# Four heads of a gated recurrence in step instead of two, in a two-layer hybrid decoder

## The chip, the core and the metric

The kernel runs on one core of one Trainium2 chip. The metric is the device time of one execution, in microseconds (us). The core has a matrix engine (TensorE, PE in the profile; its weight loads are listed as PEld), a vector engine (VectorE, DVE), a scalar engine (ScalarE, ACT), a general engine (GpSimd, POOL) and a queue that issues transfers (SyncE, SP). Each takes its own instructions in order, and they wait for one another through semaphores. SBUF is the memory that all of them read; PSUM is what TensorE writes, eight banks of 512 fp32 columns in 128 partitions.

## What is computed

Two layers over 512 tokens of width 1024. Each layer normalises its input, projects it to 6400 columns, runs two groups of heads side by side, gates both with SiLU, projects back and adds:

```python
h = rms_norm(x, g_pre)
q_h, f_h, i_h, z_h, q_a, k_a, v_a, z_a = jnp.split(h @ w_in, SPLIT_POINTS, axis=-1)
o_h = hgrn2(q_h, f_h, i_h, lb)                  # 8 heads, state 128 x 128
o_h = rms_norm(o_h, g_head) * jax.nn.silu(z_h)
o_a = sliding_window_attention(rotary(q_a), rotary(k_a), v_a, sinks) * jax.nn.silu(z_a)
x = x + rms_norm(jnp.concatenate([o_h, o_a]) @ w_out, g_post)
```

The recurrence of a head, which the change touches, is

```python
f = lb + (1 - lb) * sigmoid(f_logit);  k = 1 - f;  q = silu(q)
S_t = diag(f_t) S_{t-1} + k_t i_t^T;   o_t = S_t^T q_t
```

Everything is fp32. The large matmuls split each operand into a high and a low part and add three products.

## The kernel before

**Projections.** The weight columns come in slabs of 512: QA (2 slabs, attention queries), IV (2, the recurrence's i), FQ (4; slab FQ+p holds f and q of heads 2p and 2p+1), ZA and ZH (2 each, the gates), and the output weights in four parts a0, a1, h0, h1. `ORDER` gives their order in a layer. Each slab is cut into units that accumulate in one PSUM bank each (`pj`, three banks). A unit of an input slab has 8 steps, one of an output slab 4; a step is three 128x512 matmuls at L282. Two units run at a time, step by step in turn; `begins` says when the next one may start. When a unit ends, its `evac` reads the bank: for FQ, sigmoid, its complement and two scalings per f head (L646 to L649) and a SiLU per q head (L655); for ZA, SiLU (L798), product with the attention output (L799), high part (L800), low part (L801).

**Weights.** Each piece of 128x512 is loaded through SP's queue (L156), its high part made by ScalarE (L176), its low part by VectorE (L177; a few by GpSimd). `plan_conversions` walks the units ahead of time and gives each piece the step at which it is due.

**The recurrence.** `hgrn(a)` does the pair of heads a and a+1. It first prepares both: reciprocals, products, copies (L671 to L681). Then come six levels, for blocks of hh = 2, 4, ..., 64 tokens. In a level TensorE multiplies q of the right half of each block with k of the left half, in small matmuls that write 32 or 64 partitions each (L703 for hh up to 16, L709 for 32, L714 for 64; each is two instructions in the profile, since fp32 takes two passes). Then VectorE scales q (L720), GpSimd scales k (L721), both by the running products `tots`, and the results are kept in the score tile A: masked copies on VectorE for hh up to 16 (L732), ScalarE copies above. The diagonal blocks of two tokens (L690, kept at L727) go in with the first level. After the levels k is transposed (L750), chunk states are summed (L760 to L764), and the outputs are made (L772, L775) and normalised (L778 to L782). `a_tiles`, two score tiles cleared once at the start, serve all pairs.

**Order.** `merge` interleaves the recurrence with projection steps in the program: a stream advances when it has done the smaller share of its total. The recurrence's generator yields weights, 28.5 in all per pair (`HG_N`): 3.5 per prepared head, 2.0 or 2.5 per level, 2.0 after the transposes, 1.5 per state, 2.0 per output. The four pairs are merged with the slabs up to FQ+1, FQ+2, a1 and h0. The compiler then orders each engine's instructions by readiness; small matmuls are pinned (`pin`) behind everything written before them on TensorE, large ones are not. `sc()` hands out three PSUM banks in turn for the recurrence's and attention's scores, `ac()` two more for states and outputs. SBUF tiles come from pools by tag: `fk` has 8 tiles for f and k, `q` 4 for pairs of q, `b` and `a` 2 of double width, `s` 3, `u` 1.

Of the kernel before, what the change touches and what calls it, by code (L numbers as in the profile page):

```python
# [17 lines left out]
D_MODEL = 1024  # L18
# [11 lines left out]
QA, IV, FQ, ZA, ZH = 0, 2, 4, 8, 10  # L30
FEATURE = (0, 1, 4, 5, 6, 7, 8, 9)
# [3 lines left out]
HG_N = 28.5  # L35
# [32 lines left out]
def hybrid_kernel(ctx: ExitStack, tc: tile.TileContext, x, wkv, win, wout, g_pre, g_post, lbp, ghead, sinks,  # L68
# [19 lines left out]
    sc_turn = [0]  # L88
# [5 lines left out]
    def ac():  # L94
        return ps.tile([P, 512], F32, tag="ac", name="ac", bufs=8 - PJ - SC)
# [28 lines left out]
    ORDER = ["kv", QA, QA + 1, IV, IV + 1, FQ, ZA, FQ + 1, "a0", FQ + 2, ZA + 1, FQ + 3, "a1", ZH, "h0", ZH + 1, "h1"]  # L124
# [301 lines left out]
    def layer(l, last):  # L426
# [213 lines left out]
        def fq_stream(p):  # L640
            def evac(m, o):
                h = 2 * p + m % 2
                if m < 2:
                    f = big.tile([P, 512], F32, tag="fk", name="f", bufs=FB)
                    k = big.tile([P, 512], F32, tag="fk", name="k", bufs=FB)
                    nc.scalar.activation(f, o, AF.Sigmoid)  # L646
                    nc.scalar.activation(k, o, AF.Sigmoid, scale=-1.0)
                    nc.scalar.activation(f, f, AF.Identity, scale=lb_a[:, l, h:h + 1], bias=lb_b[:, l, h:h + 1])
                    nc.scalar.activation(k, k, AF.Identity, scale=lb_a[:, l, h:h + 1], bias=lb_c[:, l, h:h + 1])  # L649
                    fT[h], kT[h] = f, k  # L650
                else:
                    if m == 2:
                        qT["t"] = big.tile([P, 2, 512], F32, tag="q", name="q", bufs=QB)
                    qT[h] = qT["t"][:, m - 2]
                    nc.scalar.activation(qT[h], o, AF.Silu)  # L655
# [6 lines left out]
        def hgrn(a):  # L662
            hs = [(j, fT.pop(a + j), kT.pop(a + j), qT.pop(a + j), a_tiles[j]) for j in range(2)]
            blocks = lambda t, w: t.rearrange("p (b j) -> p b j", j=w)
            qbs, kbs, tots = [], [], []
            for j, f, k, q, A in hs:
# [3 lines left out]
                re = halves("a")[0][:, 0:256]  # L670
                nc.vector.reciprocal(re, f2[:, :, 1])  # L671
# [3 lines left out]
                nc.vector.tensor_tensor(kb2[:, :, 1], k2[:, :, 1], re, op=ALU.mult)  # L675
                qbs.append(qb)
                kbs.append(kb)
# [4 lines left out]
                tots.append(f2[:, :, 0])  # L682
                yield 3.5
            LBs = []
            for j in range(2):
                LB = sc()
                for n in range(NT):
                    for b in range(4):
                        c = slice(n * P + 32 * b, n * P + 32 * b + 32)
                        pin(nc.tensor.matmul(LB[32 * b:32 * b + 32, c], lhsT=kbs[j][:, c], rhs=qbs[j][:, c], start=True, stop=True,  # L690
                                             tile_position=(0, 32 * b)))
                LBs.append(LB)
            for hh in (2, 4, 8, 16, 32, 64):
                nb = SEQ // (2 * hh)
                per, qu = nb // NT, nb // NT // 4
                L = sc()
                for j, f, k, q, A in hs:
                    qv = q.rearrange("p (b two j) -> p b two j", two=2, j=hh)
                    if hh <= 16:
                        for n in range(NT):  # L700
                            for b in range(4):
                                o_, blk, c = n * P + 32 * b, n * per + b * qu, 256 * j + n * 64 + 16 * b
                                pin(nc.tensor.matmul(L[32 * b:32 * b + 32, c:c + 16], lhsT=k[:, o_:o_ + 32],  # L703
                                                 rhs=qv[:, blk:blk + qu, 1, :], start=True, stop=True, tile_position=(0, 32 * b)))
                    elif hh == 32:
                        for n in range(NT):
                            for b in range(2):
                                o_, r_, c = n * P + 64 * b, 64 * b + 32 * (n % 2), 64 * j + n // 2 * 32
                                pin(nc.tensor.matmul(L[r_:r_ + 32, c:c + 32], lhsT=k[:, o_:o_ + 32],  # L709
                                                 rhs=q[:, o_ + 32:o_ + 64], start=True, stop=True, tile_position=(0, r_)))  # L710
                    else:
                        for n in range(NT):
                            o_, b, c = n * P, n % 2, 128 * j + n // 2 * 64
                            pin(nc.tensor.matmul(L[64 * b:64 * b + 64, c:c + 64], lhsT=k[:, o_:o_ + 64],  # L714
                                             rhs=q[:, o_ + 64:o_ + 128], start=True, stop=True))
                for j, f, k, q, A in hs:
                    qv = q.rearrange("p (b two j) -> p b two j", two=2, j=hh)
                    kv_ = k.rearrange("p (b two j) -> p b two j", two=2, j=hh)
                    tv = tots[j].rearrange("p (b two) -> p b two", two=2)
                    nc.vector.tensor_tensor(qv[:, :, 1, :], qv[:, :, 1, :], tv[:, :, 0].unsqueeze(2).broadcast_to([P, nb, hh]), op=ALU.mult)  # L720
                    nc.gpsimd.tensor_tensor(kv_[:, :, 0, :], kv_[:, :, 0, :], tv[:, :, 1].unsqueeze(2).broadcast_to([P, nb, hh]), op=ALU.mult)  # L721
                    t2 = sm.tile([P, nb], F32, tag=f"tot{hh}", name=f"tot{hh}", bufs=2)
                    nc.vector.tensor_tensor(t2, tv[:, :, 0], tv[:, :, 1], op=ALU.mult)
                    tots[j] = t2
                for j, f, k, q, A in hs:
                    if hh == 2:
                        nc.vector.copy_predicated(A.rearrange("p (n t) -> p n t", n=NT), bmask.unsqueeze(1).broadcast_to([P, NT, P]),  # L727
                                                  LBs[j].rearrange("p (n t) -> p n t", n=NT))
                    if hh <= 16:
                        Av = A.rearrange("p (n b two j) -> p n b two j", n=NT, two=2, j=hh)[:, :, :, 1, :]  # L730
                        mv = lmask[hh].rearrange("p (b j) -> p b j", j=hh).unsqueeze(1).broadcast_to([P, NT, per, hh])
                        nc.vector.copy_predicated(Av, mv, L[:, 256 * j:256 * j + 256].rearrange("p (n b j) -> p n b j", n=NT, j=hh))  # L732
                    elif hh == 32:
                        Av = A.rearrange("p (m two t) -> p m two t", m=NT // 2, two=2)
                        for b in range(2):
                            for i in range(2):
                                nc.scalar.copy(Av[64 * b:64 * b + 32, :, i, 64 * b + 32:64 * b + 64],
                                               L[64 * b + 32 * i:64 * b + 32 * i + 32, 64 * j:64 * j + 64].rearrange("p (m t) -> p m t", m=NT // 2))
                    else:
                        Av = A.rearrange("p (m b t) -> p m b t", m=NT // 2, b=2)  # L740
                        for b in range(2):
                            nc.scalar.copy(Av[0:64, :, b, 64:128],
                                           L[64 * b:64 * b + 64, 128 * j:128 * j + 128].rearrange("p (m t) -> p m t", m=NT // 2))
                yield 2.5 if hh == 2 else 2.0

            kps = []
            for j, f, k, q, A in hs:
# [6 lines left out]
            yield 2.0  # L754
            vs = lambda j, n: vt[a // 4, n][:, (a % 4 + j) * P:(a % 4 + j + 1) * P]
            sts = []
            for j, f, k, q, A in hs:
# [5 lines left out]
                for n in range(1, NT - 1):  # L763
                    nc.vector.scalar_tensor_tensor(st[:, n], st[:, n - 1], tots[j][:, n:n + 1], SU[:, n * P:(n + 1) * P],  # L764
                                                   op0=ALU.mult, op1=ALU.add)
                sts.append(st)
                yield 1.5
            for j, f, k, q, A in hs:
# [15 lines left out]
                yield 2.0  # L784
# [128 lines left out]
        def run():  # L913
            hg = lambda a: (hgrn(a), HG_N)
# [110 lines left out]
    a_tiles = [const.tile([P, 512], F32, name=f"a_st{i}") for i in range(2)]  # L1025
# [4 lines left out]
    def constants():  # L1030
# [10 lines left out]
        for t in a_tiles:  # L1041
            pin(nc.gpsimd.memset(t, 0.0))
# [41 lines left out]
def _layout(inp):  # L1084
# [6 lines left out]
    fq = np.stack([f_h.reshape(DEPTH, D_MODEL, 4, 256), q_h.reshape(DEPTH, D_MODEL, 4, 256)], axis=3).reshape(DEPTH, D_MODEL, 2048)  # L1091
# [28 lines left out]
```

## Time and profile before

| | |
|---|---|
| median of 3 runs | 934.13 us (933.86 to 934.25) |
| profiled execution | 933.88 us, its span 932.1 us |
| PE busy | 910.0 us, 98% |
| DVE, ACT, POOL busy | 72%, 50%, 29% |
| granted TensorE clock, mean | 0.994 |
| large matmuls (L282), share of the chain that ended last | 71% |

The span is the time from the first to the last instruction. A row of the timeline has the start, the time from the start to the last end of its merged instructions, engine, line, operation, tiles (out<-in), shape, and xcount. Matmuls are pipelined, so one starts before the last has ended, and the spacing of starts tells what each costs. A row of a group has the busy time, the mean of one in ns, and the idle time before, with what ended it.

### The profile page before, as it was taken

The page shows a single profiled execution, that of the slowest core. Times are in us where ns is not written, and L with a number is a line of the kernel's source. Part 1 is how long each engine was busy: PE and PEld are TensorE (multiplying, and loading weights), DVE is VectorE, ACT ScalarE, POOL GpSimd, SP SyncE. Part 2 cuts the span into 40 slices and gives each one's busy share as a digit, 9 for nine tenths or more (in the row PEclk, how much of TensorE's full clock was granted, in tenths as well). Part 3 has the DMA queues.
Part 4 walks back from the last instruction along what each step waited for, and adds up shares of the span by engine and source line. Part 5 has one row for each costly group of instructions (what it writes and reads, how often), then busy time and mean ns, then how long its engine had stood idle before and what let it go on. Part 6 is the DMA issues. An engine that isn't in the chain of part 4 may idle for free.

```text
span 932.1 us, 18970 instructions
## 1 busy us (share of the span) xinstructions
PE 910.0 (98%) x7240; PEld 753.3 (81%) x7240; DVE 670.9 (72%) x1326; ACT 462.8 (50%) x1100; POOL 271.5 (29%) x286
## 2 busy tenths in 40 slices
PE   8998999999999999999989989999999999999996
PEld 7886888878788788788878868888787887887885
DVE  5978777885766783955786788677877577749556
ACT  5535658636464451444453456684554736325242
POOL 3435444232221311311232345441323212113102
PEclk9999999999999999999999989999999999999998
DMA  7685413322222142424356554123223223323313
GB/s 221 193 226 156 124 39 101 91 82 80 68 85 96 62 141 64 138 69 123 111 162 179 171 159 136 35 82 101 70 79 89 71 80 105 111 69 93 91 34 135
DMA packets 56570, 100.74 MB, mean 108 GB/s; under 512 B 6560, under 2 KB 9120, under 8 KB 56480
## 3 DMA queue, kind: packets, MB, share of 16 engines
q1 hardware_dynamic: 56192, 99.40, 35.7%
q8 instruction: 57, 0.93, 0.4%
q14 instruction: 33, 0.27, 0.1%
q10 hardware_dynamic: 288, 0.14, 0.1%
HBM read 86.93 MB, written 12.58 MB: 107 GB/s over the span
## 4 chain that ended last, share of the span: by engine, by line
PE 86%; DVE 6%; ACT 3%; POOL 2%; issue 2%; DMA 1%; SPq 0%; POOLq 0%; DVEq 0%; ACTq 0%
PE pj L282 71%; PE ac L595 2%; PE sc L703 2%; PE sc L542 2%; PE ac L772 2%; ACT s L556 1%; PE ac L775 1%; PE ac L760 1%; PE sc L569 1%; DVE wlo L177 1%; PE sc L820 1%; POOL r L343 1%; PE sc L750 1%; PE sc L714 1%; DVE a L896 1%
## 5 line engine op out<-in xcount | busy, mean ns | idle before, releaser
L282 PE MATMUL pj<-hhi,wlo 128*128 128x512 f32 x512 | 205.8, 402 | 0.0
L177 DVE TENSOR_TENSOR wlo<-raw,whi 128x512 fp32r<-128x512 f32 x249 | 182.9, 748 | 30.0 <-ACT whi L176 28.5
L282 PE MATMUL pj<-hhi,whi 128*128 128x512 f32 x512 | 200.0, 391 | 0.0
L282 PE MATMUL pj<-hlo,whi 128*128 128x512 f32 x512 | 199.5, 390 | 0.0
L176 ACT CAST whi<-raw 128x512 fp32r<-128x512 f32 x256 | 154.5, 621 | 87.9 <-PE pj L282 74.7
L282 PE MATMUL pj<-whi,ops 128*128 128x512 f32 (+1 forms) x520 | 173.5, 395 | 0.0
L282 PEld LDWEIGHTS pj<-whi,ops 128*128 128x128 f32 x520 | 97.2, 188 | 19.6
L282 PEld LDWEIGHTS pj<-hhi,whi 128*128 128x128 f32 x512 | 96.1, 188 | 20.9
L282 PEld LDWEIGHTS pj<-hhi,wlo 128*128 128x128 f32 x512 | 96.2, 188 | 18.7
L282 PEld LDWEIGHTS pj<-hlo,whi 128*128 128x128 f32 x512 | 96.3, 188 | 18.0
L282 PE MATMUL pj<-whi,hlo 128*128 128x512 f32 x256 | 104.5, 408 | 0.7 <-ACT whi L176 0.7
L282 PE MATMUL pj<-wlo,hhi 128*128 128x512 f32 x256 | 101.0, 395 | 2.0 <-DVE wlo L177 2.0
L282 PE MATMUL pj<-whi,hhi 128*128 128x512 f32 x256 | 101.0, 394 | 0.0
L282 PE MATMUL pj<-wlo,ops 128*128 128x512 f32 (+1 forms) x260 | 100.5, 386 | 0.0
L721 POOL TENSOR_TENSOR k<-k,tot 128x256 f32<-128x256 f32 x80 | 64.2, 822 | 109.4 <-PE sc L703 60.7
L556 ACT ACTIVATE s<-sc,negm 128x128 f32<-128x128 f32 x128 | 45.4, 368 | 36.8 <-DVE negm L550 26.1
L720 DVE TENSOR_TENSOR q<-q,tot 128x256 f32<-128x256 f32 x80 | 50.6, 665 | 14.6 <-PE sc L703 9.4
L282 PEld LDWEIGHTS pj<-wlo,hhi 128*128 128x128 f32 x256 | 48.8, 191 | 10.7 <-DVE wlo L177 2.3
L282 PEld LDWEIGHTS pj<-whi,hhi 128*128 128x128 f32 x256 | 48.6, 190 | 10.6
L282 PEld LDWEIGHTS pj<-whi,hlo 128*128 128x128 f32 x256 | 48.6, 190 | 9.6 <-ACT whi L176 1.1
L282 PEld LDWEIGHTS pj<-wlo,ops 128*128 128x128 f32 x260 | 49.0, 188 | 8.7
L563 POOL TENSOR_TENSOR s<-s,sums 128x512 f32<-128x512 f32 x32 | 35.8, 1119 | 57.0 <-ACT a L328 28.4
(185 smaller groups left out, 1418.7 us busy)
## 6 DMA issues: line engine op xcount, KB each, us to landing
raw<-in_win_dram SPq DMA_DIRECT2D x192, 256.0 KB, 2.7
raw<-in_wout_dram SPq DMA_DIRECT2D x64, 256.0 KB, 2.7
stack<-rot SPq DMA_DIRECT2D x16, 512.0 KB, 3.6
qs<-stack SPq DMA_DIRECT2D x32, 256.0 KB, 4.9
a<-in_x_dram SPq DMA_DIRECT2D x12, 256.0 KB, 3.1
raw<-in_wkv_dram SPq DMA_DIRECT2D x8, 256.0 KB, 3.7
x_mid<-a SPq DMA_DIRECT2D x8, 256.0 KB, 2.3
a<-x_mid SPq DMA_DIRECT2D x8, 256.0 KB, 3.0
```

The costliest lines, as they stand in the source:

```text
L176: keep(nc.scalar.copy(hi, v))
L177: keep((nc.gpsimd if i in on_pool and i % 2 else nc.vector).tensor_tensor(lo, v, hi.bitcast(F32), op=ALU.subtract))
L282: nc.tensor.matmul(u.o, lhsT=u.sta(k, u.w)[i], rhs=u.mov(k, u.w)[j], start=(n == 0), stop=(n == len(u.list) - 1))
L343: keep(nc.gpsimd.tensor_tensor(r, t, mhalf[:, 0:1], op=ALU.pow))
L542: pin(nc.tensor.matmul(S[:, h * 256:(h + 1) * 256], lhsT=q[:, 2 * hp_ + h, t_], rhs=kst[v][p][:, (n - 1) * P:(n + 1) * P], start=(h == 0 a ...
L556: nc.scalar.activation(pt[:, h * P:(h + 1) * P], cur[h], AF.Exp, bias=negm[:, h:h + 1], scale=SCALE, accum_out=sums[:, h:h + 1])
L563: nc.gpsimd.tensor_tensor(pv, pv, sums.unsqueeze(2).broadcast_to([P, 4, P]), op=ALU.mult)
L595: pin(nc.tensor.matmul(U, lhsT=vst[v][:, blk, :], rhs=d, start=(i == 0), stop=(i == len(terms) - 1)))
L703: pin(nc.tensor.matmul(L[32 * b:32 * b + 32, c:c + 16], lhsT=k[:, o_:o_ + 32], rhs=qv[:, blk:blk + qu, 1, :], start=True, stop=True, tile_ ...
L720: nc.vector.tensor_tensor(qv[:, :, 1, :], qv[:, :, 1, :], tv[:, :, 0].unsqueeze(2).broadcast_to([P, nb, hh]), op=ALU.mult)
L721: nc.gpsimd.tensor_tensor(kv_[:, :, 0, :], kv_[:, :, 0, :], tv[:, :, 1].unsqueeze(2).broadcast_to([P, nb, hh]), op=ALU.mult)
L772: pin(nc.tensor.matmul(O[:, c], lhsT=A[:, c], rhs=vs(j, n), start=(n == 0), stop=False))
```

## The change

The recurrence is cut into `prepare(a)`, which prepares two heads, and `hgrn(a)`, which takes four heads, a to a+3, through the levels. In each level the small matmuls of all four heads are issued together, into two banks of `sc()`; then heads a and a+1 are scaled and kept, then, after a yield, a+2 and a+3. A half-level has weight 3.0. The diagonal blocks of a group's first two heads are issued and kept at the end of their `prepare`, those of the other two at the start of `hgrn`. The transposes, states and outputs are issued for four heads, states and outputs interleaved.

So that four heads' inputs are there, FQ+1 comes right after FQ, and the order of the later slabs shifts: FQ, FQ+1, ZA, FQ+2, a0, FQ+3, ZA+1, a1. In FQ+2 the q half comes ahead of the f half (`Q_FIRST`, with the weight columns laid out accordingly). Since a1 now follows ZA+1, whose results it needs, `begins` lets a1's first unit start only when no other is running, and its second at once beside it.

The score tiles come from tag `a`, one double tile per pair, cleared by GpSimd in `prepare`; `a_tiles` is gone. The reciprocal is written where the scaled k will stand, and multiplied there. `ac()` hands out two fixed banks in turn. The `tot` tiles have four buffers instead of two.

```diff
-HG_N = 28.5
+HG_N = 52.0
-    ORDER = ["kv", QA, QA + 1, IV, IV + 1, FQ, ZA, FQ + 1, "a0", FQ + 2, ZA + 1, FQ + 3, "a1", ZH, "h0", ZH + 1, "h1"]
+    ORDER = ["kv", QA, QA + 1, IV, IV + 1, FQ, FQ + 1, ZA, FQ + 2, "a0", FQ + 3, ZA + 1, "a1", ZH, "h0", ZH + 1, "h1"]
...
+            self.joint = m == 1 if key[0] == "out" and key[2] == "a1" and m < 2 else None
...
+        if active and units and units[0].joint is not None:
+            return len(active) == 1 and units[0].joint and active[0].joint is False
...
-                if m < 2:
+                if (m < 2) != (p in Q_FIRST):
...
+        def prepare(a):
+
+            t = tmp("a", n=2)
+            nc.gpsimd.memset(t, 0.0)
+            for j in range(a, a + 2):
+                As[j] = t[:, j - a]
+                f, k, q = quad[j] = fT.pop(j), kT.pop(j), qT.pop(j)
...
-                nc.vector.reciprocal(re, f2[:, :, 1])
+                nc.vector.reciprocal(kb2[:, :, 1], f2[:, :, 1])
...
+            if a % 4 == 0:
+                banks = [sc(), sc()]
+                for i in range(2):
+                    spread(a + i, banks[i])
+                for i in range(2):
+                    keep_spread(a + i, banks[i])
+
+        def hgrn(a):
+            hs = [(j, *quad.pop(a + j)) for j in range(4)]
+            banks = [ac(), ac()]
+            for i in range(2):
+                spread(a + 2 + i, banks[i])
             for hh in (2, 4, 8, 16, 32, 64):
-                L = sc()
-                for j, f, k, q, A in hs:
+                Ls = [sc(), sc()]
+                for j, f, k, q in hs:
+                    L, i = Ls[j // 2], j % 2
...
+                for two in (hs[:2], hs[2:]):
+                    for j, f, k, q in two:
...
+                    yield 3.0
...
+            for fn, j, w in ((states, 0, 1.5), (states, 1, 1.5), (outputs, 0, 2.0), (states, 2, 1.5), (outputs, 1, 2.0),
+                             (states, 3, 1.5), (outputs, 2, 2.0), (outputs, 3, 2.0)):
+                fn(j)
+                yield w
...
-            merge(hg(0), rest(("in", l, FQ + 1)))
-            merge(hg(2), rest(("in", l, FQ + 2)))
-            merge(hg(4), rest(("out", l, "a1")))
-            merge(hg(6), rest(("out", l, "h0")))
+            merge((prepare(0), 7.0), rest(("in", l, FQ + 1)))
+            merge((chain(prepare(2), hgrn(0), prepare(4)), HG_N + 14), rest(("in", l, FQ + 3)))
+            merge((chain(prepare(6), hgrn(4)), HG_N + 7), rest(("out", l, "h0")))
```

More of the change, by code (lines that the diff above doesn't have):

```diff
@@ L87, in hybrid_kernel @@
     sc_tiles = [ps.tile([P, 512], F32, tag=f"sc{i}", name=f"sc{i}", bufs=1) for i in range(SC)]
-    sc_turn = [0]
+    ac_tiles = [ps.tile([P, 512], F32, tag=f"ac{i}", name=f"ac{i}", bufs=1) for i in range(8 - PJ - SC)]
+    sc_turn, ac_turn = [0], [0]
     def sc():
@@ L94, in ac @@
     def ac():
[L95 removed]
+        ac_turn[0] += 1
+        return ac_tiles[ac_turn[0] % len(ac_tiles)]
     def tmp(tag, dt=F32, n=1):
@@ L660, in layer, with spread, keep_spread @@
         on = {}
-        def hgrn(a):
-            hs = [(j, fT.pop(a + j), kT.pop(a + j), qT.pop(a + j), a_tiles[j]) for j in range(2)]
+        As, kbs, qbs, tots, quad = {}, {}, {}, {}, {}
+        def spread(j, bank):
+            for n in range(NT):
+                for b in range(4):
+                    c = slice(n * P + 32 * b, n * P + 32 * b + 32)
+                    pin(nc.tensor.matmul(bank[32 * b:32 * b + 32, c], lhsT=kbs[j][:, c], rhs=qbs[j][:, c], start=True, stop=True,
+                                         tile_position=(0, 32 * b)))
+        def keep_spread(j, bank):
+            nc.vector.copy_predicated(As[j].rearrange("p (n t) -> p n t", n=NT), bmask.unsqueeze(1).broadcast_to([P, NT, P]),
+                                      bank.rearrange("p (n t) -> p n t", n=NT))
+        def prepare(a):
+            t = tmp("a", n=2)
+            nc.gpsimd.memset(t, 0.0)
             blocks = lambda t, w: t.rearrange("p (b j) -> p b j", j=w)
-            qbs, kbs, tots = [], [], []
-            for j, f, k, q, A in hs:
+            for j in range(a, a + 2):
+                As[j] = t[:, j - a]
+                f, k, q = quad[j] = fT.pop(j), kT.pop(j), qT.pop(j)
                 f2, k2, q2 = (blocks(t, 2) for t in (f, k, q))
@@ L681, in hgrn @@
                 nc.vector.tensor_tensor(f2[:, :, 0], f2[:, :, 0], f2[:, :, 1], op=ALU.mult)
-                tots.append(f2[:, :, 0])
+                tots[j] = f2[:, :, 0]
                 yield 3.5
[L684 to L692, printed above, removed]
+            if a % 4 == 0:
[9 more added lines that the diff above has]
+                spread(a + 2 + i, banks[i])
             for hh in (2, 4, 8, 16, 32, 64):
@@ L701, in hgrn @@
                             for b in range(4):
-                                o_, blk, c = n * P + 32 * b, n * per + b * qu, 256 * j + n * 64 + 16 * b
+                                o_, blk, c = n * P + 32 * b, n * per + b * qu, 256 * i + n * 64 + 16 * b
                                 pin(nc.tensor.matmul(L[32 * b:32 * b + 32, c:c + 16], lhsT=k[:, o_:o_ + 32],
-                                                 rhs=qv[:, blk:blk + qu, 1, :], start=True, stop=True, tile_position=(0, 32 * b)))
+                                                     rhs=qv[:, blk:blk + qu, 1, :], start=True, stop=True, tile_position=(0, 32 * b)))
                     elif hh == 32:
@@ L707, in hgrn @@
                             for b in range(2):
-                                o_, r_, c = n * P + 64 * b, 64 * b + 32 * (n % 2), 64 * j + n // 2 * 32
+                                o_, r_, c = n * P + 64 * b, 64 * b + 32 * (n % 2), 64 * i + n // 2 * 32
                                 pin(nc.tensor.matmul(L[r_:r_ + 32, c:c + 32], lhsT=k[:, o_:o_ + 32],
-                                                 rhs=q[:, o_ + 32:o_ + 64], start=True, stop=True, tile_position=(0, r_)))
+                                                     rhs=q[:, o_ + 32:o_ + 64], start=True, stop=True, tile_position=(0, r_)))
@@ L711, in hgrn @@
                     else:
                         for n in range(NT):
-                            o_, b, c = n * P, n % 2, 128 * j + n // 2 * 64
+                            o_, b, c = n * P, n % 2, 128 * i + n // 2 * 64
                             pin(nc.tensor.matmul(L[64 * b:64 * b + 64, c:c + 64], lhsT=k[:, o_:o_ + 64],
[L715 to L743, printed above, removed]
@@ L744, in hgrn @@
-                yield 2.5 if hh == 2 else 2.0
+                                                 rhs=q[:, o_ + 64:o_ + 128], start=True, stop=True))
+                for two in (hs[:2], hs[2:]):
+                    for j, f, k, q in two:
+                        qv = q.rearrange("p (b two j) -> p b two j", two=2, j=hh)
+                        kv_ = k.rearrange("p (b two j) -> p b two j", two=2, j=hh)
+                        tv = tots[a + j].rearrange("p (b two) -> p b two", two=2)
+                        nc.vector.tensor_tensor(qv[:, :, 1, :], qv[:, :, 1, :], tv[:, :, 0].unsqueeze(2).broadcast_to([P, nb, hh]), op=ALU.mult)
+                        nc.gpsimd.tensor_tensor(kv_[:, :, 0, :], kv_[:, :, 0, :], tv[:, :, 1].unsqueeze(2).broadcast_to([P, nb, hh]), op=ALU.mult)
+                        t2 = sm.tile([P, nb], F32, tag=f"tot{hh}", name=f"tot{hh}", bufs=4)
+                        nc.vector.tensor_tensor(t2, tv[:, :, 0], tv[:, :, 1], op=ALU.mult)
+                        tots[a + j] = t2
+                    for j, f, k, q in two:
+                        A, L, i = As[a + j], Ls[j // 2], j % 2
+                        if hh == 2 and j >= 2:
+                            keep_spread(a + j, banks[i])
+                        if hh <= 16:
+                            Av = A.rearrange("p (n b two j) -> p n b two j", n=NT, two=2, j=hh)[:, :, :, 1, :]
+                            mv = lmask[hh].rearrange("p (b j) -> p b j", j=hh).unsqueeze(1).broadcast_to([P, NT, per, hh])
+                            nc.vector.copy_predicated(Av, mv, L[:, 256 * i:256 * i + 256].rearrange("p (n b j) -> p n b j", n=NT, j=hh))
+                        elif hh == 32:
+                            Av = A.rearrange("p (m two t) -> p m two t", m=NT // 2, two=2)
+                            for b in range(2):
+                                for e in range(2):
+                                    nc.scalar.copy(Av[64 * b:64 * b + 32, :, e, 64 * b + 32:64 * b + 64],
+                                                   L[64 * b + 32 * e:64 * b + 32 * e + 32, 64 * i:64 * i + 64].rearrange("p (m t) -> p m t", m=NT // 2))
+                        else:
+                            Av = A.rearrange("p (m b t) -> p m b t", m=NT // 2, b=2)
+                            for b in range(2):
+                                nc.scalar.copy(Av[0:64, :, b, 64:128],
+                                               L[64 * b:64 * b + 64, 128 * i:128 * i + 128].rearrange("p (m t) -> p m t", m=NT // 2))
+                    yield 3.0
@@ L746, in hgrn @@
             kps = []
-            for j, f, k, q, A in hs:
+            for j, f, k, q in hs:
                 KP = sc()
@@ L753, in hgrn, with states @@
                 kps.append(kst_)
[L754 to L757, printed above, removed]
+                if j % 2:
+                    yield 1.0
+            vs = lambda j, n: vt[a // 4, n][:, j * P:(j + 1) * P]
+            sts = {}
+            def states(j):
                 SU = ac()
@@ L763, in hgrn, with outputs @@
                 for n in range(1, NT - 1):
-                    nc.vector.scalar_tensor_tensor(st[:, n], st[:, n - 1], tots[j][:, n:n + 1], SU[:, n * P:(n + 1) * P],
+                    nc.vector.scalar_tensor_tensor(st[:, n], st[:, n - 1], tots[a + j][:, n:n + 1], SU[:, n * P:(n + 1) * P],
                                                    op0=ALU.mult, op1=ALU.add)
-                sts.append(st)
-                yield 1.5
-            for j, f, k, q, A in hs:
+                sts[j] = st
+            def outputs(j):
+                q, A = hs[j][3], As[a + j]
                 O = ac()
@@ L1024, in hybrid_kernel @@
     nsnk = const.tile([P, DEPTH, ATT_HEADS], F32, name="nsnk")
-    a_tiles = [const.tile([P, 512], F32, name=f"a_st{i}") for i in range(2)]
     lp = const.tile([P, DEPTH * HEADS], F32, name="lp")
@@ L1090, in _layout @@
     qa = q_a.reshape(DEPTH, D_MODEL, 4, 4, 2, 32).transpose(0, 1, 2, 4, 3, 5).reshape(DEPTH, D_MODEL, 1024)
-    fq = np.stack([f_h.reshape(DEPTH, D_MODEL, 4, 256), q_h.reshape(DEPTH, D_MODEL, 4, 256)], axis=3).reshape(DEPTH, D_MODEL, 2048)
+    fq = np.stack([f_h.reshape(DEPTH, D_MODEL, 4, 256), q_h.reshape(DEPTH, D_MODEL, 4, 256)], axis=3)
+    for p in Q_FIRST:
+        fq[:, :, p] = fq[:, :, p, ::-1].copy()
+    fq = fq.reshape(DEPTH, D_MODEL, 2048)
     win = np.concatenate([qa, i_h, fq, z_a, z_h], axis=2)
```

16 lines of the change are left out of this document (5 added, 11 removed).

## The prediction

> **What bounds the kernel now.** I read the page first: the busy shares and the clock.
>
> ```profile
> span 932.1 us, 18970 instructions
> ...
> PE 910.0 (98%) x7240; PEld 753.3 (81%) x7240; DVE 670.9 (72%) x1326; ACT 462.8 (50%) x1100; POOL 271.5 (29%) x286
> ...
> PEclk9999999999999999999999989999999999999998
> ```
>
> TensorE (PE) is busy for 98% of the span at nearly full clock. Next I read the busy times of a stretch of the recurrence (heads 0 and 1 of the first layer), and the list of waits.
>
> ```profile
> core 0: us, PE busy (x) PEld busy (x) DVE busy (x) ACT busy (x) POOL busy (x), PEclk, DMA share, GB/s
> 186.00:231.00 45.00, 45.00 (x566) 36.83 (x564) 32.81 (x53) 23.76 (x51) 13.82 (x17) 1.00 0.27 78
> ```
> ```profile
> PE sc L703 <- DVE ops L823: 0.3, 2, 0.2
> ```
>
> Here PE never idles, and of the recurrence's own matmuls only two waits show, 0.3 us together. VectorE has a quarter of this stretch free, GpSimd more than two thirds. So faster operands buy nothing here. What can still be won is time inside PE's stream: how closely its matmuls follow one another. The timeline of PE around one level of two heads shows that.
>
> ```profile
> 201.13 0.39 PE L282 MATMUL pj<-hhi,whi 128*128 128x512 f32 x1
> 201.45 0.74 PE L703 MATMUL sc<-q,k 128*32 128x16 f32 x64
> ...
> 202.00 0.18 PE L703 MATMUL sc<-q,k 128*32 128x16 f32 x1
> 202.12 0.50 PE L282 MATMUL pj<-hhi,wlo 128*128 128x512 f32 x1
> 202.45 0.39 PE L282 MATMUL pj<-hlo,whi 128*128 128x512 f32 x1
> 202.68 0.40 PE L282 MATMUL pj<-hhi,whi 128*128 128x512 f32 x1
> ```
>
> Starts, not durations, give the price, since matmuls overlap. Large matmuls start 0.23 us apart (202.45 to 202.68). A step of a projection is three of them, 0.69 us. The row at 202.00 is the last of the 64 small ones. From 201.13 to 202.45 there are 1.32 us, where two spacings would be 0.46: the burst costs 0.86. The 64 small starts take 0.55 of that (201.45 to 202.00). The other 0.31 is paid once per burst: 0.09 on the way in (0.32 instead of 0.23), 0.12 from the last small start to the next large one, 0.10 at the second large one (0.33 instead of 0.23).
>
> Does a second group, in another bank, pay it again? The trace has a burst with two groups:
>
> ```profile
> 188.27 0.39 PE L282 MATMUL pj<-hhi,whi 128*128 128x512 f32 x1
> 188.59 0.75 PE L690 MATMUL sc<-b 128*32 128x32 f32 x63
> ...
> 189.16 0.77 PE L703 MATMUL sc<-q,k 128*32 128x16 f32 x63
> 189.87 0.50 PE L282 MATMUL pj<-hhi,wlo 128*128 128x512 f32 x1
> 190.20 0.39 PE L282 MATMUL pj<-hlo,whi 128*128 128x512 f32 x1
> ```
>
> The 64 of L703 start right behind those of L690, without a gap. The whole costs 190.20 - 188.27 - 0.46 = 1.47 us, so the 64 of L690 added 0.61 to the 0.86 and no second 0.31. The other two kinds of level:
>
> ```profile
> 205.44 0.39 PE L282 MATMUL pj<-hhi,whi 128*128 128x512 f32 x1
> 205.75 0.46 PE L709 MATMUL sc<-q,k 128*32 128x32 f32 x32
> 206.15 0.50 PE L282 MATMUL pj<-hhi,wlo 128*128 128x512 f32 x1
> 206.48 0.39 PE L282 MATMUL pj<-hlo,whi 128*128 128x512 f32 x1
> ...
> 208.78 0.39 PE L282 MATMUL pj<-hhi,whi 128*128 128x512 f32 x1
> 209.09 0.69 PE L714 MATMUL sc<-q,k 128*64 128x64 f32 x16
> 209.71 0.50 PE L282 MATMUL pj<-hhi,wlo 128*128 128x512 f32 x1
> 210.05 0.39 PE L282 MATMUL pj<-hlo,whi 128*128 128x512 f32 x1
> ```
>
> L709 costs 0.58; by L690's price its 32 are 0.31, which leaves 0.27. L714 costs 0.81, with the same 0.08 and 0.11 at its ends. So the fixed part is some 0.3 in all three.
>
> **The change, part by part.** *Bursts.* PE gets the same matmuls. Per layer the old code has 4 pairs of heads x 6 levels = 24 bursts; the new one has 2 groups of four x 6 = 12. It also takes the L690 matmuls of heads 0 and 1 of a group out of the first level and issues them at the end of prepare: one new burst per group. Net 12 - 2 = 10 bursts fewer per layer, 20 in all: 20 x 0.31 = 6.2 us. Bounds: 3.8 us if only entry and exit (0.19) go, because the 0.12 is the last matmul's own time; 7.4 if the new burst lands beside another one (24 x 0.31). I take 6.2, because the two-group burst saves the whole.
>
> A rule of the Trainium skill speaks against this: TensorE: Matmul & The Clock Gate, section "Wait — 56ns, not 53.3ns?", says that starts never come closer than about 25 ns, however few columns a matmul has. By it, the 64 matmuls moved into a shared burst would alone take 1.6 us. This trace disagrees: 64 of them start within 0.55 us, four column tiles side by side, 9 ns apart on average. By the rule's figure the twelve joined L703 bursts would cost 12.6 us more than I reckon, and the time would be 940.9.
>
> *Levels in step.* A level's VectorE work for a pair must be done before the next burst:
>
> ```profile
> 194.19 0.74 PE L703 MATMUL sc<-q,k 128*32 128x16 f32 x64
> ...
> 197.82 0.74 PE L703 MATMUL sc<-q,k 128*32 128x16 f32 x64
> ```
> ```profile
> 195.41 1.71 DVE L720 TENSOR_TENSOR q<-q,tot 128x256 f32<-128x256 f32 x2
> 197.05 0.75 DVE L732 COPY_PREDICATED a_st<-masks,sc 128x256 f32<-128x256 uint8 x2
> ```
>
> Today q is ready at 197.12, 0.7 us before its burst; the two rows are 2.4 us of VectorE work. In the first new merge 66 units of weight lie over 4 slabs of 32 steps: 1.94 steps per unit. A level is 2 x 3.0 units, 11.6 steps, 8.0 us, in place of 3.6 per pair: two pairs' 4.8 us fit, and the second half alone has 4.0. Cost 0; without that cover the burst would be cut in two, 0.31 each, 6.2 at most. GpSimd's share is smaller:
>
> ```profile
> L721 POOL TENSOR_TENSOR k<-k,tot 128x256 f32<-128x256 f32 x80 | 64.2, 822 | 109.4 <-PE sc L703 60.7 <-PE sc L714 20.8 <-PE sc L709 20.2
> ```
>
> Four heads are 3.3 us of 8.0. The A tiles are now cleared for each pair: 8 memsets of 1024 columns, each at most the 1.6 us that twice an L721 of 256 columns takes, on an engine that is 71% idle; ahead of them stands nothing that PE needs soon, since the last products of a prepare are long done today (180.24 against the burst at 188.59):
>
> ```profile
> 180.24 0.69 DVE L680 TENSOR_TENSOR q<-b,f 128x512 f32<-128x512 f32 x1
> ```
>
> *Buffers.* Eight f and k tiles serve four heads at once. The four f come free after the first level (about step 25 of the merge) and FQ+2 wants them at about step 58, because its q half comes first; the k come free at about step 84 and FQ+3 wants them at about 108. No wait. The outputs use two banks in turn, so an output reuses a bank 3.5 units (4.7 us) after the one before:
>
> ```profile
> 223.03 0.83 PE L775 MATMUL ac<-st,q 128*128 128x128 f32 x6
> ...
> 226.66 0.69 DVE L782 TENSOR_TENSOR q<-ac,hrr 128x512 f32<-128x512 f32 x1 [1.44 <-POOL hrr L335]
> ```
>
> The bank is held from 223.86 to 227.35, 3.5 us. Cost 0.
>
> *Slabs.* The same weights come through the same queue, SP's, in another order; their due steps are counted anew. With q first in FQ+2, silu follows silu and sigmoid sigmoid, so 2 of 8 ScalarE table loads per layer fall away, off the path:
>
> ```profile
> L646 ACT ACT_TABLE_LOAD x8 | 10.3, 1283 | 9.5 <-PE pj L282 9.5
> L655 ACT ACT_TABLE_LOAD x8 | 10.3, 1283 | 0.1
> ```
>
> What is new on the path: a1 now follows ZA+1 directly, and its fourth step of K needs what ZA+1's last unit has just made.
>
> ```profile
> 305.39 0.60 ACT L798 ACTIVATE z<-pj 128x512 f32<-128x512 f32 x1 [4.85 <-PE pj L282]
> 307.38 0.72 DVE L799 TENSOR_TENSOR z<-z,oa 128x512 f32<-128x512 f32 x1
> 308.13 0.63 ACT L800 CAST ops<-z 128x512 fp32r<-128x512 f32 x1 [1.12 <-DVE z L799]
> 309.21 0.69 DVE L801 TENSOR_TENSOR ops<-z,ops 128x512 fp32r<-128x512 f32 x1
> ```
>
> This chain takes 4.5 us (305.39 to 309.90): 2.6 of work in its four rows and 1.9 between them, 1.4 of that ahead of L799. Two units of a1 in step give 6 steps of cover, 4.1 us, of which some 0.2 is the last matmul's end. So PE stands 0 to 0.6 us per layer; I take 0.2, 0.4 in all. Behind the waiting matmul stands all of PE.
>
> *Sum.* The profiled execution's own time is 933.88 (span 932.1). 933.88 - 6.2 + 0.4 = 928.1. The median of the runs is 0.25 higher: 928.3 on its footing.
>
> **Rivals.**
> 1. *Part of the bursts come apart*, because heads 2 and 3 are late and large matmuls, which are not held in order, slip between. For it: q is only 0.7 us early today. Against: each half has more time than before. With half of the 20: -3.1 + 0.4, 931.4.
> 2. *No gain*: the 0.31 is paid again at each change of bank. Against: the two-group burst. 934.1.
> 3. *Slower*: the start of a1 becomes the bound. If both VectorE steps of the chain queue behind a pair's level work (2.4 us each, in place of the 1.9), it takes 2.6 + 4.8 = 7.4 us, 3.5 beyond the cover, and the units behind a1 find no free bank of the three, so PE stands: 7.0 in two layers, 934.1 - 6.2 + 7.0 = 934.9; with a weight conversion (L177, below) ahead of each as well, 937.9. From 3.1 us per layer the gain is gone; from about 4.0 on, the change is measurably slower. Against: VectorE has a quarter free.
>
> ```profile
> L177 DVE TENSOR_TENSOR wlo<-raw,whi 128x512 fp32r<-128x512 f32 x249 | 182.9, 748 | 30.0 <-ACT whi L176 28.5
> ```
> 4. *Long bursts start more slowly.* The widest spacing of small starts is L714's: 16 in 0.62 us less the 0.12 at the end, 31 ns. If the 64 that join an L703 burst started so, they would take 2.0 us in place of 0.55, twelve times: 17.4 us more, 945.7. Against: in the two-group burst 128 starts keep the pace of 64.
>
> **How the numbers follow.** A measurement of this kernel tells about 0.2%, 1.9 us, from no change. Likeliest, all or most of the bursts joined (926 to 930.5): 0.60. Rival 1 (930.5 to 933): 0.15. Rival 2: 0.08. Rival 3: 0.13, of which 0.05 within 0.2%. Rival 4: 0.01. The remaining 0.03 is more gain than reckoned, below 926. Faster by over 0.2% (below 932.3): 0.60 + 0.03 + 0.11 of rival 1 = 0.74. Within: 0.04 + 0.08 + 0.05 = 0.17. Slower: 0.08 + 0.01 = 0.09. The range begins at 925.8, where the upper bound of the bursts (7.4) comes with no wait at a1 and 0.9 us beside, and goes to 934.2, so that rival 2 lies in it; rivals 3 and 4 and the tail below lie outside, 0.17 together.
>
> **What would show it.** L703 rows of x128 (or two of x64 back to back) between large matmuls, with about 1.42 us for the whole (0.86 + 0.55); 20 bursts fewer; 12 table loads of the two kinds in place of 16; large matmuls unchanged at 0.23 us apart. For rival 1, rows of L282 between two of L703 a step apart. For rival 3, a wait of PE at L282 for ops of L800 or L801 after ZA+1. I am wrong if joined bursts stand in the trace and each costs as much as two.

## The result, and the profile after

The changed kernel takes 936.0 us (median of 14 runs, 933.2 to 938.7) against 933.9 for the kernel before (14 runs, 932.0 to 935.5). The ratio is 1.0028, 95% interval 1.0016 to 1.0040: slower by 0.3%, where I had forecast 928.3. Its profiled execution took 935.1 us, with a span of 933.4.

Part of the difference goes with the granted clock of TensorE (1 is full speed). The changed kernel's runs go from 933.2 us at a mean granted clock of 0.996 to 938.7 at 0.988, and the median of their clocks is 0.9925. 25 runs of the kernel before, taken beside the first experiments (median 933.9 us), have 0.995. A straight line through the runs of each gives 934.8 and 933.7 us at 0.995. By this estimate about half of the difference is left at the same clock.

The page after: busy times and clock are nearly those of before.

```profile
span 933.4 us, 18982 instructions
...
PE 905.5 (97%) x7240; PEld 754.0 (81%) x7240; DVE 663.0 (71%) x1326; ACT 457.4 (49%) x1096; POOL 274.3 (29%) x292
```

The list of what PE waited for has lines that were not there:

```profile
PE sc L729 <- issue: 4.7, 2, 2.4
...
PE pj L289 <- ACT k L654: 0.7, 2, 0.4
...
PE pj L289 <- DVE ops L835: 0.6, 2, 0.3
```

(L729 is the former L703, L676 the former L690, L735 and L740 the former L709 and L714, L289 the former L282.) First the part that went as forecast, in the timeline of PE: one level of four heads.

```profile
229.93 0.39 PE L289 MATMUL pj<-hhi,whi 128*128 128x512 f32 x1
230.25 1.34 PE L729 MATMUL sc<-q,k 128*32 128x16 f32 x128
231.52 0.50 PE L289 MATMUL pj<-hhi,wlo 128*128 128x512 f32 x1
231.85 0.40 PE L289 MATMUL pj<-hlo,whi 128*128 128x512 f32 x1
```

The burst costs 231.85 - 229.93 - 0.46 = 1.46 us, where two of the old ones cost 1.72. Then the part that did not: the first level of the second group of heads, where the diagonal matmuls of heads 2 and 3 stand right ahead of the level's own.

```profile
320.22 0.39 PE L289 MATMUL pj<-hhi,whi 128*128 128x512 f32 x1
320.54 0.75 PE L676 MATMUL ac<-b 128*32 128x32 f32 x63
...
321.11 1.29 PE L729 MATMUL sc<-q,k 128*32 128x16 f32 x117
324.77 0.27 PE L729 MATMUL sc<-q,k 128*32 128x16 f32 x10 [2.37 <-issue]
324.97 0.50 PE L289 MATMUL pj<-hhi,wlo 128*128 128x512 f32 x1
325.31 0.39 PE L289 MATMUL pj<-hlo,whi 128*128 128x512 f32 x1
```

After 182 of 192 small matmuls PE stands still for 2.37 us. "issue" means that no semaphore and no transfer of data that the profile shows ended the wait. The third group's first level has the same stop (2.30 us); the first and the fourth have none and cost 2.07 us.

Here is what PE's bursts of the recurrence cost in both profiled executions, worked out from the starts of the large matmuls around them as in the prediction (us):

```text
level        before              after
first        8 bursts   12.6     4 of 64 alone 3.6; 4 of 192: 2.07, 4.63, 4.56, 2.07
4, 8, 16     24         20.7     12            17.7
32           8           4.7     4              3.8
64           8           6.5     4              5.1
sum                     44.5                   43.5, of it 5.1 in the two stops
```

Without the two stops the bursts would cost 38.4: 6.1 us less than before, against 6.2 forecast. Of the 6.1, 0.7 are two waits inside first bursts of before (PE sc L703 <- DVE ops L823, 0.33 each by the spacing of starts), which are gone; joining the bursts saved some 5.4, 0.27 per burst. The stops give back 5.1. Four waits of a large matmul, about 0.5 us each, are new as well (the last two lines of the list above, counted by the spacing of starts). Together this is -6.1 + 5.1 + 2.0 = +1.0, against 1.2 between the two profiled executions. One item is missing in this sum: 11 large matmuls here start 0.43 us after the one ahead of them instead of 0.23, against 7 in the kernel before, some 0.8 us more. With it the sum is 0.6 us too high, and that stays unexplained.

What ended a stop? The trace also records the transfers that bring TensorE's instructions, which no view of the waits lists. The page counts them:

```profile
q8 instruction: 57, 0.93, 0.4%
```

57 packets of 16 KiB for 7240 matmuls and 7240 weight loads: one for every 256 instructions or so. (The two experiments below with 128 and 1024 instructions of TensorE more have 58 and 61 packets.) The packet that was under way in each stop (start, landing, end of the stop, us):

```text
second group:  322.04   323.35   324.77
third group:   672.04   673.35   674.61
```

In both, PE went on 1.3 to 1.4 us after the packet had landed. A burst of 192 small matmuls has 384 instructions with its weight loads, and takes some 1.9 us from the first start to the next large matmul (the unstopped groups): PE can run through more than a whole block of instructions while the next one is still coming. That was my theory for the experiments; the rival was that an operand or a semaphore of the first level comes late.

The trace holds one more sign. Count TensorE's instructions in order of time (matmuls, weight loads and the few of its sequencer): 5057 come before the one that ends the second group's stop, 9921 before the one that ends the third's. Both numbers leave 193 when divided by 256. For the ten stops of the experiments below the remainder is 193 or 194 as well. So every stop falls at the same place in a block of 256 instructions, whatever the instruction there is.

### The profile page after: what moved, and what is told of

It reads as the page before. It is cut to its first block, busy times and chain, and to the rows that moved or that the text cites. A ratio compares the mean times of both kernels' runs of the same rounds, so it can differ in the third digit from the quotient of the medians.

```text
span 933.4 us, 18982 instructions
## 1 busy us (share of the span) xinstructions
PE 905.5 (97%) x7240; PEld 754.0 (81%) x7240; DVE 663.0 (71%) x1326; ACT 457.4 (49%) x1096; POOL 274.3 (29%) x292
## 4 chain that ended last, share of the span: by engine, by line
PE 78%; DVE 10%; ACT 5%; issue 3%; POOL 2%; DMA 1%; POOLq 0%; DVEq 0%; ACTq 0%
PE pj L289 64%; PE ac L602 2%; DVE wlo L180 2%; PE sc L549 2%; PE sc L729 2%; PE ac L802 2%; ACT s L563 1%; PE ac L805 1%; PE ac L789 1%; PE sc L576 1%; PE sc L854 1%; DVE q L747 1%; ACT whi L179 1%; POOL r L350 1%; ACT a L764 1%
## 5 line engine op out<-in xcount | busy, mean ns | idle before, releaser
L289 PE MATMUL pj<-hhi,wlo 128*128 128x512 f32 x512 | 204.5, 399 | 0.0
L289 PE MATMUL pj<-hhi,whi 128*128 128x512 f32 x512 | 200.3, 391 | 0.0
L289 PE MATMUL pj<-hlo,whi 128*128 128x512 f32 x512 | 200.2, 391 | 0.0
L289 PE MATMUL pj<-whi,ops 128*128 128x512 f32 (+1 forms) x520 | 174.3, 396 | 1.3 <-ACT k L654 0.7
L289 PEld LDWEIGHTS pj<-whi,ops 128*128 128x128 f32 x520 | 97.3, 188 | 22.1 <-ACT k L654 1.5
L289 PEld LDWEIGHTS pj<-hhi,whi 128*128 128x128 f32 x512 | 96.5, 189 | 20.8
L289 PEld LDWEIGHTS pj<-hhi,wlo 128*128 128x128 f32 x512 | 96.5, 188 | 19.0
L289 PEld LDWEIGHTS pj<-hlo,whi 128*128 128x128 f32 x512 | 96.7, 189 | 18.5
L289 PE MATMUL pj<-whi,hlo 128*128 128x512 f32 x256 | 104.2, 407 | 0.7 <-ACT whi L179 0.7
L289 PE MATMUL pj<-wlo,hhi 128*128 128x512 f32 x256 | 100.3, 392 | 2.0 <-DVE wlo L180 2.0
L289 PE MATMUL pj<-wlo,ops 128*128 128x512 f32 (+1 forms) x260 | 100.5, 387 | 0.0
L289 PE MATMUL pj<-whi,hhi 128*128 128x512 f32 x256 | 100.5, 393 | 0.0
L289 PEld LDWEIGHTS pj<-wlo,hhi 128*128 128x128 f32 x256 | 48.6, 190 | 10.7 <-DVE wlo L180 2.3
L289 PEld LDWEIGHTS pj<-whi,hhi 128*128 128x128 f32 x256 | 48.2, 188 | 10.6
L289 PEld LDWEIGHTS pj<-whi,hlo 128*128 128x128 f32 x256 | 48.5, 189 | 9.5 <-ACT whi L179 1.1
L289 PEld LDWEIGHTS pj<-wlo,ops 128*128 128x128 f32 x260 | 49.0, 188 | 8.5
```

Source lines behind the costliest of these rows:

```text
L289: nc.tensor.matmul(u.o, lhsT=u.sta(k, u.w)[i], rhs=u.mov(k, u.w)[j], start=(n == 0), stop=(n == len(u.list) - 1))
```

## Experiments

**Apart.** One yield between the diagonal matmuls and the first level.

```diff
             for i in range(2):
                 spread(a + 2 + i, banks[i])
+            yield 1.0
-HG_N = 52.0
+HG_N = 53.0
```

> The changed kernel with one yield of weight 1.0 between the diagonal matmuls of heads 2 and 3 and the first level, so that no burst has more than 128 small matmuls (256 instructions with their weight loads) instead of 192 (384). Theory (TensorE runs out of fetched instructions inside the burst of 192): no wait of 2.3 us by 'issue' is left in any first level, the burst costs about 1.46 and the split-off one 0.89, together 0.28 more than the unstalled 2.07, four times 1.1 us; two stalls of 2.5 us and the slow matmuls behind one of them go: 5 to 6.7 us less. Net 4 to 5.5 us below the changed kernel, 930.5 to 932. Rival (the wait belongs to an operand or a semaphore of the first level): the wait stays in front of or inside the first level of the same groups, and the time is at or above the changed kernel's 936.

Measured: 931.3 us (12 runs, 929.8 to 934.5), ratio to the kernel before 0.9982 (0.9971 to 0.9994). The time is as the theory said, but the stops were not all gone, so this is luck in part: by the spacing of starts 2.4 us of them stayed, while the waits for ops at a1, 0.9 us in two layers, went without being forecast. The stops got shorter, in the same two groups:

```profile
668.11 0.76 PE L676 MATMUL ac<-b 128*32 128x32 f32 x64
...
669.70 1.27 PE L730 MATMUL sc<-q,k 128*32 128x16 f32 x119
672.46 0.27 PE L730 MATMUL sc<-q,k 128*32 128x16 f32 x9 [1.49 <-issue]
```

So it isn't the length of one burst that decides. What counts is how many instructions PE eats within the time that a block takes to come: the 64 diagonal matmuls 1.6 us earlier count as well. The packet of this stop landed at 671.00, 1.46 us before the end.

**Shifted.** The changed kernel with 128 instructions of TensorE more at the start, nothing else.

```diff
     pin(nc.tensor.matmul(warm, lhsT=ones[:, 0:P], rhs=ones, start=True, stop=True))
+    for _ in range(32):
+        pin(nc.tensor.matmul(warm[0:32, 0:32], lhsT=ones[:, 0:32], rhs=ones[:, 0:32], start=True, stop=True, tile_position=(0, 0)))
```

> The changed kernel with 32 small matmuls more (128 instructions of TensorE) in its first microseconds, where TensorE waits for the first loads; nothing else. Theory (instruction fetch in blocks): the place of the block boundaries moves by half a block against every burst, so the waits of 2.3 us by 'issue' change place: other first levels stall (the changed kernel has them in the second and third of four), or their number changes by one or two, 2.5 us each; time 933 to 939 by their number. Rival (operand or semaphore): the same two first levels stall as in the changed kernel, at the same small matmul, and the time is the same within its interval.

Measured: 936.8 us (6 runs, 935.8 to 937.0), ratio 1.0029 (1.0018 to 1.0040). The waits of PE and the two places in its timeline:

```profile
PE sc L729 <- issue: 2.2, 1, 2.2
...
PE pj L289 <- issue: 0.9, 1, 0.9
```
```profile
217.23 0.40 PE L289 MATMUL pj<-hlo,whi 128*128 128x512 f32 x1
218.52 0.50 PE L289 MATMUL pj<-hhi,whi 128*128 128x512 f32 x1 [0.90 <-issue]
...
782.30 1.22 PE L729 MATMUL sc<-q,k 128*32 128x16 f32 x108
785.68 0.37 PE L729 MATMUL sc<-q,k 128*32 128x16 f32 x19 [2.16 <-issue]
```

The second and third group, which stopped before, now run through; the fourth stops inside its burst, and the first 1 us behind its burst, at a large matmul that takes part in nothing of the recurrence. The stops moved with the place of the blocks, while operands, semaphores and order stayed. This rules out the rival. The stop at 218.52 also shows that the instruction that comes late need not be a small matmul.

**Doubled.** The second level's matmuls twice in a row, 512 instructions in a burst; it computes the same.

```diff
-                        for n in range(NT):
+                        for n in [n for n in range(NT) for _ in range(2 if hh == 4 else 1)]:
```

> The changed kernel with the small matmuls of the second level (hh = 4) issued twice in a row, 256 in a burst (512 instructions) instead of 128; the result is the same. Theory (instruction fetch): these four bursts, which never stall in the changed kernel, now cost 1.12 us more for the matmuls and most of them stall by about 2.3 us as well, 2.6 to 3.6 us more each on average; time 944 to 950. Rival (the stall belongs to the first level's operands): they cost 1.12 us more each and no stall, 4.5 us in all, about 940.5.

Measured: 953.2 us (2 runs), 3 above the range that the theory had given. Three of the four doubled bursts stop, and one of the four stops just behind it:

```profile
PE sc L729 <- issue: 11.5, 5, 2.7
...
PE pj L289 <- issue: 1.4, 1, 1.4
```
```profile
339.87 2.08 PE L729 MATMUL sc<-q,k 128*32 128x16 f32 x205
344.09 0.93 PE L729 MATMUL sc<-q,k 128*32 128x16 f32 x51 [2.15 <-issue]
344.95 0.80 PE L289 MATMUL pj<-hhi,wlo 128*128 128x512 f32 x1
345.55 0.63 PE L289 MATMUL pj<-hlo,whi 128*128 128x512 f32 x1
345.98 0.63 PE L289 MATMUL pj<-hhi,whi 128*128 128x512 f32 x1
346.40 0.63 PE L289 MATMUL pj<-whi,ops 128*128 128x512 f32 x1
```

A level that never stopped does so once its burst is long enough. The rows behind it show what the range had missed: for a while the large matmuls start 0.43 us apart instead of 0.23. The granted clock (PEclk) was 0.50 there:

```profile
core 0: us, PE busy (x) PEld busy (x) DVE busy (x) ACT busy (x) POOL busy (x), PEclk, DMA share, GB/s
343.75:347.16 3.41, 3.07 (x56) 2.65 (x56) 1.11 (x3) 0.46 (x1) 0.86 (x1) 0.50 0.03 5
```

This execution has five such stretches of 3.41 us ahead of its last microseconds. Each begins between 0.4 us before and 1.1 us after the end of a stop. In them lie 26 starts that come 0.2 us late, against 11 in the changed kernel's execution and 7 in that of before, all at a clock of 0.50 as well. Stretches like that also stand in kernels without any stop (10 such starts in the run "cut" below), and six of the twelve stops have none behind them, so they can't be laid to the stops alone.

**Order alone.** The kernel before, with two heads in step, but with the new order of slabs, q first in FQ+2 and the joint start of a1.

```diff
-            merge(hg(0), rest(("in", l, FQ + 1)))
-            merge(hg(2), rest(("in", l, FQ + 2)))
+            merge(hg(0), rest(("in", l, ZA)))
+            merge(hg(2), rest(("out", l, "a0")))
```

> The kernel before with the new order of slabs, q first in FQ+2 and a1's joint start, but two heads in step as before; the pairs are merged with the slabs up to ZA, a0, a1 and h0 (64, 64, 96 and 64 steps, as many as before). Theory (the waits of 0.5 us at the start of a1 come from the order): a1's wait of 0.3 to 0.6 us per layer shows at L800's or L801's place, time 0.5 to 1.5 us above the kernel before. Rival (they come from four heads in step crowding VectorE and ScalarE): no such wait, time that of the kernel before within 0.5 us.

Measured: 933.8 us (10 runs, 932.0 to 934.4), ratio 0.9997 (0.9987 to 1.0007). PE waits neither for ops of the last ZA step nor for the sigmoids of FQ+2. My theory fell here: the order costs nothing by itself. The four waits of 0.5 us stand only in kernels with both the order and four heads in step, but not in all of those: by the spacing of starts "apart" and "far apart" have only the two for the sigmoids, and "cut" has none.

**Far apart.** As "apart", with weight 3.0 in place of 1.0: about 6 steps instead of 2.

> As the run with the diagonal matmuls set apart from the first level, but with weight 3.0 (about 6 steps, 4 us) between the two instead of 1.0 (2 steps). Theory (TensorE's instructions are fetched in blocks, and a second block is eaten before the next has come): with 4 us between, the waits of 0.7 and 1.7 us by 'issue' that are left in the second and third first level go; 2.4 us less than 931.3, and some slow matmuls less: 928 to 929.5. Rival (what is left belongs to the first level's operands): they stay, and the time is 931 again.

Measured: 929.7 us (6 runs, 928.4 to 931.8), ratio 0.9961 (0.9946 to 0.9976). PE's list has no wait by "issue" at these lines any more, and the second group's first level runs through:

```profile
323.04 0.76 PE L676 MATMUL ac<-b 128*32 128x32 f32 x64
...
328.06 1.34 PE L730 MATMUL sc<-q,k 128*32 128x16 f32 x128
329.33 0.50 PE L289 MATMUL pj<-hhi,wlo 128*128 128x512 f32 x1
```

The same matmuls 4 us further apart: no stop, and 6.3 us less than the changed kernel, although four bursts of 64 stand alone now that did not. In the profiled executions 3.8 of it are the bursts (39.7 against 43.5) and 1.2 the waits: those for ops are gone, those for the sigmoids 0.4 instead of 0.5 each. I did not trace the rest; the median of the runs' granted clocks is higher too, 0.995 against 0.9925.

**Cut.** As "far apart", with each level's burst cut between the two pairs of heads. This undoes the gain of the shared burst and leaves the rest.

```diff
                 for j, f, k, q in hs:
+                    if j == 2:
+                        yield 1.0
...
-                    yield 3.0
+                    yield 2.5
```

> As the one with weight 3.0 between, but each level's burst is cut in two by a yield of weight 1.0 between the matmuls of heads 0, 1 and those of heads 2, 3 (half-levels then weigh 2.5, the sum is the same). It measures the gain of the shared burst by itself. Theory (0.31 us is paid per burst): 24 bursts more, 7.4 us above the one beside it, each cut burst at 0.86, 0.58 and 0.81 us as in the kernel before. Rival (no fixed part): the same time, with two bursts of half the cost each.

Measured: 934.8 us (10 runs, 932.6 to 937.5), ratio to the kernel before 1.0014 (1.0000 to 1.0028); 5.1 above "far apart". The two halves of a cut burst:

```profile
328.09 0.39 PE L289 MATMUL pj<-hhi,whi 128*128 128x512 f32 x1
328.41 0.74 PE L732 MATMUL sc<-q,k 128*32 128x16 f32 x64
329.08 0.50 PE L289 MATMUL pj<-hhi,wlo 128*128 128x512 f32 x1
329.41 0.39 PE L289 MATMUL pj<-hlo,whi 128*128 128x512 f32 x1
```

Each costs 0.86 again (329.41 - 328.09 - 0.46), where both together cost 1.46 to 1.48. Over all the recurrence's bursts of the two profiled executions it is 46.3 us against 39.7, 6.6 more. The fixed part per burst is real, some 0.28 us, a little below the 7.4 in all that the expectation had; by the medians 5.1 of the 6.6 reach the end.

**The rest of the waits.** Two ways to take the sigmoids of FQ+2 away from the level of 32, where ScalarE makes sixteen copies: ZA+1 ahead of FQ+3, with an ordinary start of a1; or f first in FQ+2.

```diff
-    ORDER = ["kv", QA, QA + 1, IV, IV + 1, FQ, FQ + 1, ZA, FQ + 2, "a0", FQ + 3, ZA + 1, "a1", ZH, "h0", ZH + 1, "h1"]
+    ORDER = ["kv", QA, QA + 1, IV, IV + 1, FQ, FQ + 1, ZA, FQ + 2, "a0", ZA + 1, FQ + 3, "a1", ZH, "h0", ZH + 1, "h1"]
...
-            self.joint = m == 1 if key[0] == "out" and key[2] == "a1" and m < 2 else None
+            self.joint = None
```
```diff
-Q_FIRST = (2,)
+Q_FIRST = ()
```

> As the one with weight 3.0 between, and ZA+1 put ahead of FQ+3 in the order of slabs, a1 without a joint start; the first merge then has 160 steps, the second 96. Theory: the two waits of TensorE for the sigmoids of FQ+2 (0.5 us per layer), which stand where ScalarE also makes the sixteen copies of the level of 32, go, since that level comes later against the slabs: 1 us less than the one beside it. Rival: the second group's levels, now with 4.9 steps per half instead of 6.5, crowd ScalarE and VectorE and new waits of as much or more come; same time or up to 1.5 us more.

> As the one with weight 3.0 between, but FQ+2 has its f half first again (Q_FIRST empty). Theory (the wait for the sigmoids of FQ+2 comes from f falling at the level of 32): the 0.5 us per layer go, 4 table loads more on ScalarE cost nothing on the path, time about 1 us less or the same; it could wait instead for tiles of f, whose reuse then begins some 16 steps earlier, still after the first level. Rival (q first is needed): new waits of TensorE for ScalarE's evacuation of FQ+2 or FQ+3, 1 us or more above.

Measured: 928.0 us (6 runs, 927.0 to 929.4), ratio 0.9940 (0.9927 to 0.9954), for the first; 928.9 us (4 runs, 926.6 to 930.0), ratio 0.9945 (0.9928 to 0.9962), for the second. In neither does PE wait for ScalarE's k any more; "far apart" still had

```profile
PE pj L289 <- ACT k L654: 0.5, 2, 0.2
```

By the medians the gain over "far apart" is 1.7 and 0.8 us, of the size expected, but the runs of the three overlap. The first one's runs also have a higher granted clock, 0.997 in the median against 0.995; a straight line through the runs of each gives 929.4 and 929.5 us at 0.995, an estimate by which its gain goes with the clock. So it is shown that the wait went, and not what that is worth. Either beats both kernels, by 5 to 6 us against the one before and by 7 to 8 against the changed one.

## Why the prediction was wrong, point by point

**What bounds the kernel.** Right: time inside PE's stream decided, in both directions. But I read only starts that follow one another, and took it that PE always has its next instruction.

**Bursts.** The count was right and the price a little high: some 0.27 us per burst instead of 0.31, and 1.46 for a joined burst against the 1.42 that I gave. The cut run shows the fixed part by itself. That the bursts without the stops came to 6.1 us less, against 6.2, is luck in part, since 0.7 of it are two old waits. The step that failed is the one that extended the row: "I take 6.2, because the two-group burst saves the whole". That burst has 256 instructions. The new first level has 384 within 1.9 us, and there the trace of before had nothing to say. Rival 4, long bursts that start more slowly, was nearest, but with the wrong form: the pace within a burst stays, and a single stop of 2.3 to 2.4 us comes instead, in two groups of four. In the sum it was a term set at nothing, and it cost 5.1 us in the profiled execution; with the waits, 2.0 where I had 0.4, this is most of the 7.7 us between 928.3 and 936.0. I dismissed it at 0.01 with "128 starts keep the pace of 64", which says nothing of 192. I also counted twelve joined L703 bursts, in this rival and beside it, where there are sixteen: I left out the four first levels, where the loss came. The page before had a pointer, its line of the instruction queue with 16 KiB per packet; in the trace of before these packets took 0.9 to 1.9 us each, and that for each of the four first levels would have been a first estimate to put beside the 6.2.

The Trainium skill (Runtime: NRT & Kernel Launch, section "Instruction fetch mechanics") says that instructions come in blocks of 16 KiB, 256 of them, fetched through a queue of the sequencer's own, and that this is mostly hidden, because instructions are dispatched more slowly than they are filled in. The block size agrees with this trace (57 packets, 0.93 MB). That it is hidden holds for most blocks of this trace, but not at the two stops: small matmuls and their weight loads go at about 4.3 ns per instruction (128 of them in 0.55 us), and PE stood for 2.3 to 2.4 us.

**Levels in step, table loads.** Right: no wait of L729, L735 or L740 for VectorE or GpSimd is listed, and the table loads for sigmoid and SiLU fell from 16 to 12.

**Buffers and slabs.** Partly wrong. I had counted nothing for FQ+2; its last unit held its bank until ScalarE, busy with the copies of the level of 32, had read it, 0.5 us per layer:

```profile
253.58 1.71 ACT L764 COPY a<-sc 32x64 f32<-32x64 f32 x8
255.31 0.60 ACT L653 ACTIVATE f<-pj 128x512 f32<-128x512 f32 x1
255.80 0.59 ACT L654 ACTIVATE k<-pj 128x512 f32<-128x512 f32 x1
```

**The start of a1.** The mechanism was right and the size small: about 0.5 us per layer against 0.2 taken and 0.6 as the bound. That the order causes it by itself, as I had it, is wrong (order alone).

**Rivals.** Rival 1 didn't happen, all bursts stayed together. Rival 2 is refuted by the cut run. Rival 3 had the right place for a small wait and the wrong place for the loss.

## What to carry to other kernels

A price read from short bursts holds for longer ones only as far as everything that feeds them has been seen at that length; instructions are one of those things. Where TensorE can run through some 300 instructions in less than 4 us or so (in these runs 3.0 us led to a stop and 4.9 did not), look for waits that nothing in the profile ends, and set a few large matmuls between. A wait that moves when instructions are added far ahead of it points to fetching; counting the instructions up to each such wait tells whether they all fall at one place in a block.

## What was not expected of the hardware

TensorE ran out of instructions. Twelve such stops stand in the profiles of four kernels (two in the changed one, two in "apart", two in "shifted", six in "doubled"), 0.5 to 2.7 us each, and every one ended 1.2 to 1.5 us after a 16 KiB packet of instructions had landed. Which bursts stop depends on where the blocks of instructions lie: 128 instructions more at the start moved the stops from the second and third group to the fourth and behind the first.

The traces also bound how far ahead the instructions are fetched. Take the instruction at which a stop would fall, one in every 256, as the first of its packet. In all ten profiled executions, 565 blocks, no packet started more than 299 instructions ahead of it, and it never started earlier than 1.2 us after its packet had landed. Where PE took 4.9 us or more over these 299 instructions, it ran through. At the twelve stops it took 1.4 to 3.0 us over them, the stop itself not counted.

The stretches of 0.43 us between large matmuls are stretches in which the granted clock was 0.50. What brings those is open: one came with six of the twelve stops, and others stand in executions without a stop.
